# 138 matmuls and 22 transposes, read by nobody, behind a kernel's last used matmul

## The chip, the cores and the metric

The kernel runs on one core of a Trainium2 chip. The metric is the device time of one execution, in microseconds (us). Before the change two runs took 822.97 and 823.05 us, median 823.01 us. TensorE is called PE in the profile (its weight loads PEld), VectorE DVE, ScalarE ACT, GpSimd POOL, and SyncE, which issues the DMAs, SP.

## What is computed

One step of a hybrid transformer layer for a prompt of 1024 positions and for 32 sample positions with a cache of 512, all in float32, width 1024:

```
u = rmsnorm(h, g_pre) @ w_in            # 1024 x 4096: q, k, v and a gate for mixers A and B
oa = band_attention(qa, ka, va)         # 8 heads, chunks of 64, band of 8 + 1 chunks, softmax
ob = stick_breaking(qb, kb, vb)         # 8 heads, causal, products of sigmoids for weights
y = concat(oa * silu(ga), ob * silu(gb)) @ w_out
h = h + rmsnorm(y, g_post)
h = h + sigmoid(h @ w_ple_gate) * (p @ w_ple)
```

Returned are the new h of prompt and sample, and the new keys and values of both mixers. The change adds to none of these.

## The kernel before, in words

The kernel is written as a recording. Calls such as `nc.tensor.matmul` go to a `Recorder` (line 200), which notes each operation with the operations that it must follow. `Recorder.order` (line 307) then plays a model of the five engines. Each engine takes, of its operations that are ready, the one with the lowest key: for TensorE the key is the class `rec.cls` at the time of recording, and then the place in the recording. `Recorder.emit` (line 375) writes the operations in that order; so line 385, the call inside `emit`, is the source line of nearly every instruction in the profile, and the tiles' names tell them apart.

Float32 products are made of pairs: each operand is split into a high part of type float32r and a low remainder, and three float32r products (high x high, high x low, low x high) make one. The work has three stages:

- Normalisation, projection and attention. The columns of `w_in` are taken 128 at a time, against `hnh` and `hnl` (the normalised input, transposed, in three chunks of 352 positions): 24 matmuls of 352 columns for one chunk. These are the groups `mm_qA` to `mm_gB`. Attention is woven between: scores `SA` and `SB`, transposed weights `ptwA` and `ptwB`, values `PVA` and `PVB`.
- The output projection. The 1024 x 1024 product is made by a seven-product scheme on blocks of 512 x 512 (line 1346: `ORDER`, `WHICH`, `LEFT`), four passes over pairs of row tiles (line 1557). `multiply` (line 1414) is one product: 12 matmuls of 512 columns, named `o0P` to `o3P`.
- The gate product with `w_ple_gate`, in the same scheme (`g0P` to `g3P`). Its right-hand blocks are `blocks["g", key]`, float32r tiles of 128 x (2 x 4 x 512): high and low part, four slices, 512 columns. In the last pass the last product, P3 with block `B22`, is cut in two pieces of 256 columns for the second row tile (line 1588, `tail`); their PSUM tiles are `g3P` and `g3P3b`. Behind each piece VectorE adds it to `uu`, `Gate.out` (line 1463) takes the sigmoid, multiplies and adds, and SyncE issues the output DMA.

PSUM tiles come from `psum(tag, name)` (line 408), each one bank of 512 float32 columns. The tags have 2 (`mm`), 3 (`S`), 2 (`T`) and 1 (`PV`) banks. Within a tag the tiles take turns; a new tile must wait for the last use of the one whose bank it takes. `ident` (line 432) is a float32 identity of 128 x 128, which the transposes use.

At the start there are 12 matmuls of 256 columns into a tile `idle` (line 811), whose results nobody reads.

Of the kernel before, what the change touches and what calls it, by code (L numbers as in the profile page):

```python
# [13 lines left out]
P = 128  # L14
# [3 lines left out]
T = SEQ + NS  # L18
# [372 lines left out]
def stream_step(  # L391
# [6 lines left out]
    rec = Recorder()  # L398
    nc = rec
# [8 lines left out]
    def psum(tag, name):  # L408
        return ps.tile([P, 512], F32, tag=tag, name=name, bufs=PS_BUFS[tag])

    def scratch(shape, name):
# [19 lines left out]
    ident = const.tile([P, P], F32, tag="ident", name="ident")  # L431
# [7 lines left out]
        out=maskb, in_=maskb, pattern=[[-1, P]], base=0, channel_multiplier=1,  # L439
# [614 lines left out]
    for n in range(-1, 8):  # L1054
        a = len(order)
        if n < 7:
            ab, p = pairs[n + 1]
# [217 lines left out]
    blocks = {}  # L1275
# [44 lines left out]
    count = [0]  # L1320
# [236 lines left out]
    for m, (nm, src, group) in enumerate(sets):  # L1557
        last_set = m == len(sets) - 1
        state = [{}, {}]
        for n, prod in enumerate(ORDER):  # L1560
            for pair, t in enumerate(group):
# [28 lines left out]
                banks = [bank, psum("S", f"{nm}{t}{prod}b")] if tail else [bank]  # L1590
# [36 lines left out]
                else:  # L1627
                    uu = st.get("uu")
                    if prod in ("P2", "P4") and pair == 0:
                        name = f"cc{m}{prod}"  # L1630
# [31 lines left out]
        if m in (0, 2):  # L1662
# [8 lines left out]
            else:  # L1671
                for q in range(2):
                    g8 = Gate(8, HALF[q])
                    y = short_product(nm, short, q)
                    g8.out(y, at2.tile([P, 512], F32, tag="stg", name=f"o8_{q}", bufs=3))

    rec.emit(tc)


# [33 lines left out]
```

## Time and profile before

| what | value |
|---|---|
| median of two runs | 823.01 us |
| the profiled execution | 822.59 us |
| its span, first to last instruction | 820.8 us |
| PE matmuls, weight loads | 4926 of each |
| granted TensorE clock, mean | 1.000 |
| other engines' busy share | DVE 73%, POOL 62%, ACT 60% |
| HBM traffic | 81.21 MB read, 36.59 MB written |

The page of the profile gives the busy time of each engine, the span in 40 slices, the chain of work that ended last, and the costliest groups of instructions. A matmul's recorded time is longer than the distance to the next one, since matmuls are pipelined; the rate of a group is read from the starts, or from the pieces of the chain, which tile the span. In the timeline "x12" means that 12 instructions of a kind are merged into one row. Between span and device time of the profiled execution lie 1.8 us.

### The profile page before, as it was taken

What the parts mean: (1) busy time and instruction counts of PE and PEld (TensorE: products, weight loads), DVE (VectorE), ACT (ScalarE), POOL (GpSimd) and SP (SyncE); (2) the same over time, 40 slices, a digit from 0 to 9 for tenths busy, and PEclk for the clock granted to TensorE, in tenths of its full rate; (3) what the DMA queues carried; (4) which work ended last, traced back from release to release, by engine and by line L of the source; (5) the groups of instructions that cost most, each with busy time, mean ns of one, the idle gap of its engine ahead of it and who ended that gap; (6) DMA issues with size and microseconds to landing.
All of it is one profiled execution on the core that took longest, in us unless ns stands there. A gap on an engine that the chain in (4) does not pass through costs nothing.

```text
span 820.8 us, 14862 instructions
## 1 busy us (share of the span) xinstructions
PE 811.7 (99%) x4926; PEld 751.1 (92%) x4926; DVE 601.8 (73%) x1197; ACT 496.1 (60%) x1145; POOL 508.3 (62%) x559
## 2 busy tenths in 40 slices
PE   9999999999999999999999999999999999999997
PEld 7999999999999999999999999999998787888786
DVE  6718886776677688898988889985654676686755
ACT  6624745655636667756665775663437966886741
POOL 6526775585766486675657856676463437599513
PEclk9999999999999999999999999999999999999999
DMA  9327544574545563312333233253479847749733
GB/s 309 109 70 249 145 143 146 146 204 146 147 120 171 144 174 96 85 33 67 105 89 82 50 105 92 83 150 111 135 258 303 287 143 243 251 156 362 245 117 128
DMA packets 113279, 127.19 MB, mean 155 GB/s; under 512 B 10850, under 2 KB 80266, under 8 KB 113203
## 3 DMA queue, kind: packets, MB, share of 16 engines
q1 hardware_dynamic: 113202, 126.24, 50.5%
q8 instruction: 39, 0.64, 0.3%
q14 instruction: 38, 0.30, 0.1%
HBM read 81.21 MB, written 36.59 MB: 144 GB/s over the span
## 4 chain that ended last, share of the span: by engine, by line
PE 94%; DVE 2%; POOL 1%; ACT 1%; DMA 1%; issue 0%; SPq 0%; DVEq 0%
PE mm_kB L385 6%; PE mm_gA L385 6%; PE mm_qA L385 6%; PE mm_kA L385 6%; PE mm_gB L385 5%; PE mm_qB L385 5%; PE mm_vA L385 5%; PE mm_vB L385 5%; PE PVB L385 4%; PE SB L385 4%; PE ptwB L385 4%; PE SA L385 4%; PE PVA L385 4%; PE ptwA L385 3%; PE g1P L385 2%; PE o3P L385 2%
## 5 line engine op out<-in xcount | busy, mean ns | idle before, releaser
L385 POOL TENSOR_TENSOR beB<-beB,omB 128x128 f32<-128x128 f32 (+7 forms) x64 | 87.5, 1373 | 78.6 <-DVE omB L385 25.0
L385 DVE TENSOR_TENSOR_SCAN omB<-omB 128x128 f32<-128x128 f32 (+7 forms) x64 | 100.1, 1575 | 4.4 <-ACT omB L385 2.2
L385 POOL TENSOR_SCALAR beA<-beA,statA 128x640 f32<-128x640 f32 (+2 forms) x64 | 44.3, 696 | 48.6 <-DVE statA L385 47.0
L385 ACT CAST wThA<-ptwA 128x128 fp32r<-128x128 f32 (+3 forms) x96 | 40.1, 424 | 37.4 <-PE ptwA L385 36.5
L385 ACT CAST wThB<-ptwB 128x512 fp32r<-128x512 f32 (+3 forms) x96 | 44.9, 487 | 24.7 <-PE ptwB L385 23.2
L385 ACT ACTIVATE omB<-SB 128x384 f32<-128x384 f32 (+5 forms) x96 | 47.4, 507 | 18.9 <-DVE SB L385 8.1
L385 DVE TENSOR_TENSOR wTlB<-ptwB,wThB 128x512 fp32r<-128x512 f32 (+3 forms) x96 | 50.7, 547 | 9.0 <-ACT wThB L385 7.2
L385 DVE TENSOR_TENSOR wTlA<-ptwA,wThA 128x128 fp32r<-128x128 f32 (+3 forms) x96 | 45.6, 485 | 15.7 <-ACT wThA L385 15.0
L385 ACT ACTIVATE beA<-omA,statA 128x640 f32<-128x640 f32 (+2 forms) x64 | 44.7, 699 | 9.4 <-DVE statA L385 3.5
L385 ACT ACTIVATE beB<-SB 128x384 f32<-128x384 f32 (+5 forms) x96 | 46.6, 506 | 3.4 <-DVE Vl2sB L385 2.0
L385 PE MATMUL ptwB<-ident,beB 128*128 128x128 f32 x288 | 45.0, 273 | 0.1
L385 PE MATMUL ptwA<-ident,beA 128*128 128x128 f32 x240 | 41.5, 273 | 0.0
L385 PEld LDWEIGHTS ptwB<-ident,beB 128*128 128x128 f32 x288 | 35.1, 140 | 2.3 <-issue 0.4
L385 PE MATMUL SB<-kdB,LB 128*128 128x384 f32 (+5 forms) x96 | 34.1, 358 | 0.5 <-ACT beB L385 0.5
L385 DVE CUSTOM_DVE_ANT_0 omA<-SA,biasA 128x320 f32<-128x320 f32 (+2 forms) x64 | 30.8, 481 | 4.5 <-PE SA L385 3.8
L385 PE MATMUL SB<-klB,LB 128*128 128x384 f32 (+5 forms) x96 | 33.4, 349 | 0.0
L385 PEld LDWEIGHTS ptwA<-ident,beA 128*128 128x128 f32 x240 | 30.7, 140 | 1.4 <-issue 0.2
L385 POOL TENSOR_TENSOR oB<-oB,oB 128x256 f32<-128x256 f32 x32 | 25.4, 815 | 10.2 <-issue 5.6
L385 PE MATMUL SA<-kdA,LA 128*128 128x320 f32 (+2 forms) x96 | 31.2, 332 | 0.5 <-DVE LA L385 0.4
L385 POOL TENSOR_TENSOR gB<-gB,gB 128x256 f32<-128x256 f32 x32 | 27.5, 878 | 6.3 <-DMA gB<-in_w_ple_gate_dram 6.1
L385 PE MATMUL SA<-klA,LA 128*128 128x320 f32 (+2 forms) x96 | 30.4, 324 | 0.0
L385 POOL TENSOR_TENSOR h<-h,x 128x512 f32<-128x512 f32 (+1 forms) x18 | 23.4, 1320 | 0.8 <-DVE h L385 0.8
(706 smaller groups left out, 2698.1 us busy)
## 6 DMA issues: line engine op xcount, KB each, us to landing
x<-in_x_prompt_dram SPq DMA_DIRECT2D x8, 512.0 KB, 5.5
oB<-in_w_out_dram SPq DMA_DIRECT2D x16, 256.0 KB, 4.5
sum_dro<-oB SPq DMA_DIRECT2D x16, 256.0 KB, 2.2
gB<-in_w_ple_gate_dram SPq DMA_DIRECT2D x16, 256.0 KB, 4.3
sum_drg<-gB SPq DMA_DIRECT2D x16, 256.0 KB, 2.1
x<-in_x_prompt_dram SPq DMA_DIRECT2D x16, 256.0 KB, 3.8
h_dr<-h SPq DMA_DIRECT2D x8, 512.0 KB, 3.5
ht<-h_dr SPq DMA_DIRECT2D x8, 512.0 KB, 5.1
```

The costliest lines, as they stand in the source:

```text
L385: getattr(getattr(tc.nc, o.what[0]), o.what[1])(*args, **kw)
```

## The change

Ahead of `rec.emit(tc)` the recording gets 13 rows of matmuls in class 5, which no other operation has, so that TensorE takes them last. The whole diff:

```
+    rec.cls = 5
+    flat = [blocks["g", key].rearrange("p a k c -> p (a k c)") for key in ("B22", "T1")]
+
+    def twice(name):
+        pt = psum("T", name)
+        for x in range(2):
+            nc.tensor.transpose(pt[:, x * P:(x + 1) * P], ident, ident)
+
+    def row_of(name, n, base=104, step_w=P, step_m=None, banks=1, each=False, count=12, lead=True):
+        if lead:
+            twice("t" + name)
+        out = [psum("mm", f"{name}{x}") for x in range(banks)]
+        step_m = n if step_m is None else step_m
+        for i in range(count):
+            w = flat[0][:, base + step_w * (i % 8):base + step_w * (i % 8) + P]
+            m = flat[1][:, base + step_m * (i % 6):base + step_m * (i % 6) + n]
+            nc.tensor.matmul(out[i % banks][:, 0:n], w, m, start=each or i < banks, stop=each or i >= count - banks)
+
+    row_of("ra", 352)
+    row_of("rb", 352, base=0)
+    row_of("rc", 352, step_w=0)
+    row_of("rd", 352, step_m=0)
+    row_of("re", 352, step_w=0, step_m=0)
+    row_of("rf", 512)
+    row_of("rg", 512, step_w=0, step_m=0)
+    row_of("rh", 384, count=8)
+    row_of("ri", 336, count=8)
+    row_of("rj", 352, banks=2)
+    row_of("rk", 352, each=True)
+    row_of("rl", P, count=2, lead=False)
+    row_of("rm", 352, lead=False)
```

`twice` is two transposes of the identity into one bank of tag `T`; eleven of the rows begin with it. A row is `count` matmuls of `n` columns into one bank of tag `mm` (`rj`: two banks in turn), summed up over the row (`rk`: each on its own, `start` and `stop` set every time). Weights are 128 columns of block `B22`, moved on by `step_w` from one matmul to the next; the moving columns come from block `T1`, moved on by `step_m`; both start at element `base`. That makes 138 matmuls and 22 transposes. Nothing reads the banks, and no output depends on them.

## The prediction

> **What bounds the kernel now.** I read the page first, then the chain of work that ended last over the final 20 us, then the timeline of the end and the waits of the DMA queue's engine there. The changed program's instruction order was read beside them.
>
> ```profile
> span 820.8 us, 14862 instructions
> PE 811.7 (99%) x4926; PEld 751.1 (92%) x4926; DVE 601.8 (73%) x1197; ACT 496.1 (60%) x1145; POOL 508.3 (62%) x559
> PEclk9999999999999999999999999999999999999999
> PE 94%; DVE 2%; POOL 1%; ACT 1%; DMA 1%; issue 0%; SPq 0%; DVEq 0%
> ```
>
> TensorE is busy 99% of the span, makes 94% of the chain, and its granted clock is at the top digit throughout. So work appended to TensorE has no idle time to fall into, except behind the last used matmul. The chain of the last 20 us shows where that is:
>
> ```profile
> 807.65 2.80 PE g3P L385 x12
> 810.44 2.76 PE g2P L385 x12
> 813.20 1.45 PE g3P L385 x12
> 814.65 1.46 PE g3P3b L385 x12
> 816.10 0.02 issue
> 816.13 0.77 DVE uu L385 x2
> ...
> 817.79 0.42 DVE uu L385
> ```
>
> Products of 12 matmuls follow each other without a gap until 816.10; the last two are 256 columns wide. What comes behind them is VectorE's sum, a gate and the output DMA. The end of TensorE's work, and how the five engines fill the rest:
>
> ```profile
> 815.80 0.29 PE L385 MATMUL g3P3b<-gB,wlS4g 128*128 128x256 f32 x1
> 817.08 1.50 SPq L385 DMA_DIRECT2D out_dram<-uu  x3
> ...
> 816.10:820.80 4.70, 0.00 (x0) 0.00 (x0) 2.02 (x5) 0.41 (x2) 0.95 (x1) 1.00 0.33 113
> ```
>
> In the last row the columns are PE, PEld, DVE, ACT and POOL busy: TensorE does nothing in the last 4.70 us. That is the only cover in the kernel for added TensorE work. What closes the program stands in the waits of SyncE from 816 on:
>
> ```profile
> SPq L1709 <- DMA out_dram<-uu: 1.1, 3, 0.4
> SPq L1709 <- PEq L1709: 0.6, 2, 0.4
> ```
>
> SyncE waits for the last output transfers and then twice for the other engines: the program ends with a barrier that all engines, TensorE too, must reach. So matmuls whose results nobody reads still hold the end, once they outlast the transfers.
>
> **The change, part by part.** It adds 138 matmuls and 22 transposes on TensorE, in 13 rows: 11 with two transposes ahead, two (rl, rm) without. It removes nothing. In the built order the 160 stand behind the last g3P3b matmul and ahead of TensorE's closing branch. ACT, DVE, POOL and SP have the same instructions with the same waits in the same order as before; only buffer numbers moved. So there is no added DMA, no step is moved past a queue, and nothing ahead of 815.8 us changes. By width: 96 matmuls of 352 columns (ra to re, rj, rk, rm), 24 of 512 (rf, rg), 8 of 384 (rh), 8 of 336 (ri), 2 of 128 (rl).
>
> Recorded matmul durations overlap (0.29 us for a 256-column one above, but 12 of them in 1.46), so I price by distance from start to start:
>
> ```profile
> 591.07 33.19 PE mm_gB L385 x205
> 552.99 13.41 PE mm_gA L385 x83
> ```
>
> 352 columns: 33.19/205 = 0.1619 us and 13.41/83 = 0.1616 us, each with its own weight load. 96 x 0.1619 = 15.54 us.
>
> 512 columns: 2.76/12 = 0.230 and 2.80/12 = 0.233 by the chain's g2P and g3P rows. I take the middle, 0.2315: 24 x 0.2315 = 5.56 us.
>
> The TensorE page of the Trainium skill ("TensorE: Matmul & The Clock Gate", section "Back-to-back issue gap") gives N / 2.4 + 2.5 ns for one matmul behind another on the warm clock, which would be 149 ns for 352 columns and 216 for 512. This trace does not agree: 162 and 230 to 233. By that rule the whole sum would be an estimated 1.9 us smaller; I keep the trace.
>
> 384, 336 and 128 columns, from these rows of TensorE's timeline:
>
> ```profile
> 339.89 0.31 PE L385 MATMUL SB<-klB,LB 128*128 128x320 f32 x1
> 340.04 0.75 PE L385 MATMUL PVB<-wTlB,v2B 128*128 128x512 f32 x4
> ...
> 343.49 0.34 PE L385 MATMUL SB<-klB,LB 128*128 128x384 f32 x1
> 343.67 0.27 PE L385 MATMUL ptwB<-ident,beB 128*128 128x128 f32 x1
> ...
> 82.30 0.22 PE L385 MATMUL SA<-kdA,LA 128*128 128x128 f32 x1
> 82.36 0.27 PE L385 MATMUL SA<-klA,LA 128*128 128x128 f32 x1
> 82.47 0.53 PE L385 MATMUL mm_kA<-hnh,wl_kA 128*128 128x352 f32 x2
> ```
>
> 384 columns: 343.67 - 343.49 = 0.18; the line between 352 and 512 columns gives 0.176, which I take: 8 x 0.176 = 1.41 us. 336 columns lie between 320 (340.04 - 339.89 = 0.15) and 352 (0.162): 0.154, 8 x 0.154 = 1.23 us. 128 columns: 0.06 and 0.11, so 2 x 0.085 = 0.17 us.
>
> Transposes: a pair of them inside 352-column work shows the cost with what it does to the matmul behind it.
>
> ```profile
> 105.88 0.38 PE L385 MATMUL ptwA<-ident,beA 128*128 128x128 f32 x2
> 106.01 1.05 PE L385 MATMUL mm_qA<-hnl,wh_qA 128*128 128x352 f32 x5
> 106.90 0.38 PE L385 MATMUL ptwA<-ident,beA 128*128 128x128 f32 x2
> ```
>
> From 105.88 to 106.90 there are two transposes and five matmuls: 1.02 - 5 x 0.1619 = 0.21 us a pair. Start to start the pair seems to take only 0.13, but the first matmul behind it starts early and takes longer. 11 x 0.21 = 2.31 us. The lower end for a pair is that 0.13.
>
> Waits: 20 of the added instructions wait on TensorE's own semaphore, because a PSUM bank is used again and its last writer was TensorE. With two banks for each of the two tags, a row waits for the row before the last, finished some two microseconds earlier. Satisfied waits cost nothing that the trace can show: every g2P and g3P product above begins with waits on VectorE or ScalarE, and they follow each other gapless. One wait is short: rm waits for rk, and only rl's two narrow matmuls stand between. The result of a matmul is there when its recorded time ends, 0.32 us after its start (row of x1 below), against 0.17 us of rl plus 0.16 of its own slot; with the semaphore's way and a weight load (0.19) not hidden I put 0.3 us there, bounds 0 and 0.5.
>
> ```profile
> 105.72 0.32 PE L385 MATMUL mm_qA<-hnl,wh_qA 128*128 128x352 f32 x1
> 815.68 0.19 PEld L385 LDWEIGHTS g3P3b<-gB,wlS4g 128*128 128x128 f32 x1
> ```
>
> Sum: 15.54 + 5.56 + 1.41 + 1.23 + 0.17 + 2.31 + 0.30 = 26.52 us of TensorE.
>
> Rows also differ in start address (0 or 104 elements), in whether weights or moving columns stay the same, in the bank and in the start and stop flags. No row of this trace isolates any of these. The spread at one width bounds them: 0.230 to 0.233 (1.4%) at 512 columns with quite different tiles. An unaligned start could cost more than that, the same weights could save something; I allow -3% and +5% on the 138 matmuls (24 us), that is -0.7 and +1.2 us, and take 0.
>
> Where the end goes: the last used matmul starts at 815.80, and 256 columns take a slot of 1.46/12 = 0.12, so the first added one can start at 815.92. 815.92 + 26.52 = 842.44 is the end of the last slot; its result is there 0.16 later, at 842.60. Behind that comes the closing of the program. The barrier is at least the 0.6 us of the SPq row; the upper end is from the last output packet to the span's end. The DMA view of 816 to 820.8, in 40 slices of 0.12 us, shows the last packets in the 30th, at 819.6, so 1.2 us:
>
> ```profile
> DMA  8100000000000000999898999489920000000000
> ```
>
> I take 0.9 and reach 843.5. The output DMA, landed by 819.6, is no longer on the path. So 843.5 - 820.8 = +22.7 us; 3.8 us of the 26.5 are covered by the old tail.
>
> The profiled execution took 822.59 us with a span of 820.8; the same 1.8 us around the new span give 845.3. The median of the runs, 823.01, is 0.4 above the profiled one, which gives 845.7. I predict 845.6 us.
>
> **The rivals.** *Not slower, because unread matmuls do not stay in the program, or do not run.* None of the 160 results is read. If they fell away the time would be 823.0. Against it:
>
> ```profile
> L385 PE MATMUL idle<-newh x12: 415/415/582, 1.3 to 3.8; 128*128 128x256 f32 x12
> ```
>
> These 12 matmuls at the start are read by nobody either, and all 12 ran. The case decides only if some 40 or more of the 160 went away. I give 0.01.
>
> *Within 2%, because the added matmuls run closer together.* 2% of 823.0 is 16.5 us, about what a measurement of this kernel can tell from no change. With 3.8 us covered, the added work would have to take under 20.3 us, 0.77 of my price: 0.125 us for 352 columns. Rows with repeated weights, on an otherwise quiet chip, would be the place. As a floor I take the pace at which transposes, each with a 128 x 128 weight load as well, follow each other in long rows:
>
> ```profile
> 331.55 0.49 PE L385 MATMUL ptwB<-ident,beB 128*128 128x128 f32 x3
> 331.88 0.60 PE L385 MATMUL ptkB<-ident,stkB 128*128 128x128 f32 x4
> ```
>
> Three in 0.33 us, 0.11 each: 138 x 0.11 + 2.31 + 0.30 = 17.8 us, and the time would be 845.6 - 8.7 = 836.9. Against it: 33.19 us for 205 is the rate in a stretch where nothing but these products stands on the chain, and in the tail g2P runs at 0.230 while the other engines are half idle. The Trainium skill's page "TensorE: Matmul & The Clock Gate", section "Back-to-back issue gap", states that a stream of weight loads and matmuls sustains about 131 ns for each of 512 columns, below its own figure for a single one, by which this rival would hold; the trace has 230. I give 0.02.
>
> *Slower than forecast, because waits on TensorE's own semaphore are not free.* If the wait stops TensorE's sequencer so that each of the 20 exposes a matmul's rest (0.32 - 0.16 = 0.16) and a weight load (0.19), that is 20 x 0.35 = 7 us, and the time is 852.6; half of it gives 849. For it: no product in this trace waits for TensorE itself. Against it: the waits are two rows old, and the gapless products. I give 0.07.
>
> **How the numbers follow.** The forecast as summed has 0.90. Its low end: 352 columns at 0.1616, 512 at 0.230, pairs at 0.13, no wait and 0.6 of closing take off 0.03 + 0.04 + 0.88 + 0.3 + 0.3 = 1.5, and addresses 0.7: 843.4. Its high end: 0.233 for 512, the wait at 0.5, 1.2 of closing and 1.2 for addresses add 1.7, 847.3; the range reaches to the first half of the waiting rival, 849. Range 843.2 to 849.0. Slower by over 2% (above 839.5) holds the forecast and the waiting rival, 0.97; the two others make 0.025 for within 2%; faster has no mechanism, 0.005.
>
> **What would show it right or wrong.** The last g3P3b matmul should still start near 815.8 and the last output DMA still land before 820. The timeline should show 13 rows behind it: 352-column rows of 12 with transposes in about 2.15 us (12 x 0.162 + 0.21), the 512-column ones in 2.99, rm starting late by 0.3. TensorE's count should be 5086 and its last matmul end near 842.6. I am wrong if a row is off by over 5% (addresses or weights matter), if idle time stands ahead of the transposes or of a row's first matmul (waits), if the clock falls below 1.00 in the tail, or if the span ends more than 1.2 us behind the last matmul.

## The result, and the profile after

The changed kernel took 848.31 us (median of 848.21 and 848.40) against 823.01, a ratio of 1.0307 with a 95% interval of 1.0263 to 1.0352. The forecast was 845.6, its range 843.2 to 849.0. So it is slower, as forecast, and 2.7 us above the point. The profiled execution took 848.40 us.

Its page, for the span and TensorE's counts:

```profile
span 846.6 us, 15182 instructions
PE 841.1 (99%) x5086; PEld 778.9 (92%) x5086; DVE 601.1 (71%) x1197; ACT 496.5 (59%) x1145; POOL 509.0 (60%) x559
```

All 160 added instructions ran (5086 - 4926), and no other engine has one more. The chain of work that ended last, from the last used product on (start, duration, tile, count; the pieces tile the time):

```profile
817.92 1.44 PE g3P3b L385 x12
819.36 0.22 PE tra L385 x2
819.58 1.94 PE ra L385 x12
821.52 0.22 PE trb L385 x2
821.74 1.94 PE rb L385 x12
823.68 0.22 PE trc L385 x2
823.90 1.94 PE rc L385 x12
825.84 0.22 PE trd L385 x2
826.06 1.93 PE rd L385 x12
827.99 0.22 PE tre L385 x2
828.21 1.94 PE re L385 x12
830.14 0.22 PE trf L385 x2
830.36 2.73 PE rf L385 x12
833.10 0.22 PE trg L385 x2
833.32 2.75 PE rg L385 x12
836.07 0.22 PE trh L385 x2
836.29 1.41 PE rh L385 x8
837.70 0.22 PE tri L385 x2
837.91 1.23 PE ri L385 x8
839.14 0.22 PE trj L385 x2
839.36 1.94 PE rj L385 x12
841.30 0.22 PE trk L385 x2
841.52 1.94 PE rk L385 x12
843.47 0.17 PE rl L385 x2
843.64 2.10 PE rm L385 x12
```

Two things are to be seen. The rows run without a gap from 819.36 to 845.74, which is 26.38 us; the forecast had 26.52. And they begin 3.3 us later than in the trace of before, where g3P3b ended at 816.10. The last used matmul itself:

```profile
819.08 0.29 PE L385 MATMUL g3P3b<-gB,wlS4g 128*128 128x256 f32 x1
```

It starts 3.28 us behind the 815.80 of before, although nothing ahead of it was changed. Its slot of 0.12 and the rows lead to 845.57, the end of rm's slot; its result is there at 845.73, and the span ends at 846.6. SyncE now waits for rm instead of the output DMA, and the two steps of the barrier cost what they did:

```profile
SPq L1742 <- PE rm L385: 23.3, 1, 23.3
SPq L1742 <- PEq L1742: 0.6, 2, 0.4
```

Where the 3.28 us arose is seen when the starts of equal matmuls are laid side by side over both traces: the distance grows to 2.55 us in the first 27 us, jumps by 0.9 near 153 us, and shrinks by 0.2 behind that. The first stretch on TensorE, in before:

```profile
4.07 1.62 PE L385 MATMUL ptp<-ident,pp 128*128 128x128 f32 x8
5.61 1.19 PE L385 MATMUL gpre<-ghl,ones 1*128 1x512 f32 x4
6.73 2.11 PE L385 MATMUL ple<-wph0True,php 128*128 128x512 f32 x8
8.68 1.07 PE L385 MATMUL ple<-wpl0True,php 128*128 128x512 f32 x4
```

and the same four tiles and the next in after:

```profile
4.16 1.94 PE L385 MATMUL ptp<-ident,pp 128*128 128x128 f32 x8
6.03 2.07 PE L385 MATMUL gpre<-ghl,ones 1*128 1x512 f32 x4
8.03 3.78 PE L385 MATMUL ple<-wph0True,php 128*128 128x512 f32 x8
11.61 1.91 PE L385 MATMUL ple<-wpl0True,php 128*128 128x512 f32 x4
13.32 1.49 PE L385 MATMUL ple<-wph1True,php 128*128 128x512 f32 x4
```

Four matmuls of 512 columns stand from 11.61 to 13.32, 0.43 us each; in before they go from 8.68 to 9.59, 0.23 each. By the single starts the pace doubles at 5.2 us in before and at 14.2 us in after. The Trainium skill's page "TensorE: Matmul & The Clock Gate", section "What's actually happening", has a half-rate clock of 1.2 GHz as the state at rest, released by sustained activity; an estimate from that clock, one column a cycle, is 427 ns for 512 columns, and the pace of 0.427 us agrees with it. The view of the granted clock does not show it: it reads 1.00 for this stretch of after too (third column from the end; 10 matmuls where before has 18).

```profile
8.00:12.00 4.00, 4.00 (x10) 3.14 (x10) 1.19 (x3) 2.84 (x5) 1.46 (x4) 1.00 1.03 400
```

That 1.00 is no measurement. The trace of after holds no record of the clock at all; in before the first record, of the full clock, begins at 5.21 us, where the pace doubles. Where there is no record, the view prints 1.00.

The 0.9 us near 153: in after a load of projection weights came late, ScalarE stood 1.40 us at its cast, and the cast behind it held up TensorE's values product.

```profile
153.70 0.62 ACT L385 CAST wh_vA<-wr_vA 128x512 fp32r<-128x512 f32 x1 [1.40 <-DMA wr_vA<-in_w_in_dram]
...
154.92 0.67 PE L385 MATMUL PVA<-wThA,v2A 128*128 128x512 f32 x2 [0.64 <-ACT wThA L385]
```

In before the same cast waited for 0.29 us:

```profile
149.91 0.62 ACT L385 CAST wh_vA<-wr_vA 128x512 fp32r<-128x512 f32 x1 [0.29 <-DMA wr_vA<-in_w_in_dram]
```

So the question for the experiments was whether the 3.28 us belong to the change or to the execution. My theory: to the execution, since the start of the pace differs from one to the next. The rival: a longer program starts slower.

### The profile page after: what moved, and what is told of

It is laid out like the page before. It is cut to its first block, busy times and chain, and to the rows that moved or that the text cites. A ratio compares the mean times of both kernels' runs of the same rounds, so it can differ in the third digit from the quotient of the medians.

```text
span 846.6 us, 15182 instructions
## 1 busy us (share of the span) xinstructions
PE 841.1 (99%) x5086; PEld 778.9 (92%) x5086; DVE 601.1 (71%) x1197; ACT 496.5 (59%) x1145; POOL 509.0 (60%) x559
## 4 chain that ended last, share of the span: by engine, by line
PE 96%; DVE 2%; ACT 1%; DMA 1%; issue 0%; DVEq 0%
PE mm_kB L385 6%; PE mm_kA L385 6%; PE mm_gA L385 5%; PE mm_gB L385 5%; PE mm_qB L385 5%; PE mm_qA L385 5%; PE mm_vA L385 5%; PE mm_vB L385 5%; PE PVB L385 4%; PE SB L385 4%; PE ptwB L385 4%; PE PVA L385 3%; PE SA L385 3%; PE ple L385 3%; PE ptwA L385 3%; PE g1P L385 2%
## 5 line engine op out<-in xcount | busy, mean ns | idle before, releaser
L385 ACT CAST wThB<-ptwB 128x512 fp32r<-128x512 f32 (+3 forms) x96 | 44.9, 486 | 24.3 <-PE ptwB L385 22.7
L385 POOL TENSOR_TENSOR oB<-oB,oB 128x256 f32<-128x256 f32 x32 | 25.5, 818 | 11.6 <-issue 5.7
```

The costliest lines, as they stand in the source:

```text
L385: getattr(getattr(tc.nc, o.what[0]), o.what[1])(*args, **kw)
```

## The experiments

**The changed kernel again, unaltered (no edit).**

> The changed kernel once more, unaltered. In its first profile the last used matmul started 3.28 us later than in the kernel before: 2.55 us of that were lost in the first 25 us, where 512-column matmuls stood 0.427 us apart until 14.2 us (0.23 from 5.2 us on in the kernel before), and 0.8 us behind a weight load that landed late near 153 us. Theory (the start of the clock differs from execution to execution, whatever the program): the times spread over 2 us or more, between about 845.0 (22.6 us above 822.6, the price of the rows alone) and 848.5, and a profile with an early rise of the pace has its last g3P3b matmul near 815.8. Rival (the longer program itself starts slower): all executions near 848.3, within 0.3, and the profile has the slow pace until 14 us again.

Measured: 845.56, 846.19, 847.29 and 848.03 us, beside 21 runs of the kernel before on the same chip from 822.57 to 825.36, median 823.63. The ratio is 1.0277 (1.0263 to 1.0291). The spread is 2.5 us for the changed kernel and 2.8 us for the one before: the theory's case, and the two values each of the first measurement had hidden it. The profile fell on the execution of 847.29, again with the pace slow until 13.9 us, and with the last g3P3b at 817.97; near 151 us nothing came late. The rows took 26.21 us from first to last start, as before.

**One row only.**

```
     row_of("ra", 352)
-    row_of("rb", 352, base=0)
...
-    row_of("rm", 352, lead=False)
```

> Only the first of the 13 rows (two transposes, 12 matmuls of 352 columns, 2.16 us in the first profile). The old tail covers 3.8 us by the prediction, so the row itself costs 0.0 us, and the span ends with the output transfers. Theory (start of the clock varies by execution): 823.0, or up to 826.3 in executions with the late rise. Rival (any lengthening of the program delays the start): 826 in all executions. Rival (the cover is not there, since the closing waits for TensorE first): 825.2 with an early rise.

Measured: 823.35 us, ratio 0.9999 (0.9990 to 1.0008). The row of 2.16 us costs nothing. Its profile has it behind the last used matmul, and SyncE waits for the output transfers at the end, not for TensorE:

```profile
816.83 0.22 PE tra L385 x2
817.05 1.94 PE ra L385 x12
```

```profile
SPq L1730 <- DMA out_dram<-uu: 1.1, 3, 0.4
```

So the cover of the old tail is real for at least these 2.16 us. And the pace rises at 4.8 us in this lengthened program, though it falls back to the slow one from 8.2 to 11.6 us.

**36 unread matmuls at the start, with and without the rows.** Both kernels have this edit; the second is without the change.

```
-    for _ in range(12):
+    for _ in range(36):
         nc.tensor.matmul(idle[:, 0:256], newest[0][:, 0:P], newest[0][:, P:P + 256], start=True, stop=True)
```

> The changed kernel with 36 instead of 12 unread matmuls of 256 columns at the start, so that TensorE is busy without a pause for at least 6 us before its first real work. If a late rise of the pace made the 2.55 us, both kernels with 36 have the fast pace from at most 9 us on, and this one is 22.6 us (26.4 of rows less 3.8 covered) above the kernel with 36 and no rows, within 0.4; a late weight load can add up to 0.9. If the longer program starts slower for another reason, the difference stays 25.3.

> The kernel before with 36 instead of 12 unread matmuls at the start. By itself 0 to 4 us slower than the kernel before, since 24 more matmuls hold up the first transposes by 3 to 5 us and part of that is given back while TensorE waits for the input. Its use is the difference to the changed kernel with 36: 22.6 by the theory that the start made the surplus, 25.3 by the rival that the longer program did.

Measured: 846.25 us with the rows (845.44 to 847.03, five runs) and 823.73 without (822.95 to 824.28, eleven runs), against 823.63 for the kernel before; the ratios to it are 1.0272 (1.0258 to 1.0286) and 0.9996 (0.9987 to 1.0005). The two differ by 22.5 us, where the theory had 22.6 and the rival 25.3. In both profiles the pace is fast from 4.6 and 4.8 us on, and the last g3P3b starts at nearly the same time, with the rows first:

```profile
816.31 0.29 PE L385 MATMUL g3P3b<-gB,wlS4g 128*128 128x256 f32 x1
```

```profile
816.15 0.29 PE L385 MATMUL g3P3b<-gB,wlS4g 128*128 128x256 f32 x1
```

With the start made alike, the surplus is gone. A spread of 1.6 and 1.3 us is left, over fewer runs than the 2.5 and 2.8 above, so the start need not be all of it. The 24 further matmuls, some 3 us of TensorE, cost nothing that can be measured at that place.

**All rows twice.** The second set has the same 13 calls under other names.

```
     row_of("rm", 352, lead=False)
+    row_of("sa", 352)
...
+    row_of("sm", 352, lead=False)
```

> All 13 rows twice, 320 added instructions on TensorE instead of 160. The first set took 26.4 us and 3.8 of it were covered; the second finds no cover left. Theory (price per row, no other cost): rows of 52.7 us together in the profile, the time 48.9 to 49.3 us above the kernel before, that is 872.5 for a median of 823.6, with the same spread of 2 to 3 us from the start. Rival (waits on TensorE's own semaphore grow, or the program's length matters): the second set costs more than 26.4, the time above 874.5.

Measured: 872.25 us beside 823.50, ratio 1.0591 (1.0574 to 1.0609), +48.75 us; the theory had 872.5. From first to last start the rows take 52.42 us in its profile, twice 26.21. The order of a few transposes differs (three pairs of the second set moved ahead of rm), and the price does not.

**2 unread matmuls at the start, no rows.**

```
-    for _ in range(12):
+    for _ in range(2):
```

> The kernel before with 2 instead of 12 unread matmuls at the start, no rows. By the theory that a late rise of the pace made most of the surplus, this kernel has it always late (near 14 us, as in the profiles with 847.3 and 848.4) and its times are near the upper end of the kernel before, 824.5 to 826. Rival (the start is not on the path, because TensorE waits for the input there anyway): the same as before, 823.6.

Measured: 824.93 us (823.32 to 826.38) beside 823.50, ratio 1.0016 (1.0007 to 1.0026). The start is on the path, but the expectation was only half met: the times run from one end to the other, so the rise is not always late, or a late one does not always cost much. In the profile, of an execution of 823.55 us, it came at 10.8 us, and the last g3P3b started at 816.76.

**Single executions of both kernels, unaltered (no edit).**

> The kernel before, unaltered, one look. By the theory the rise of the pace comes early or late with no change to the program: a time near 823 goes with a rise near 5 us and a last g3P3b near 816, a time above 824.5 with a rise near 14 us and a last g3P3b near 818. Rival (the rise is late only in the longer programs): a rise near 5 us whatever the time.

> The same once more, for another look at the start: an early rise with a time near 823, or a late one with a time above 824.5; by the rival always an early one.

> The changed kernel, unaltered, one look. Both of its profiles so far had a late rise of the pace (13.9 and 14.2 us), all seven of other programs an early one or, with 2 unread matmuls, one at 10.8. By the theory an early rise comes here too: then the last g3P3b starts near 816.2, the rows take the same 26.2 us from first to last start, and the time is near 845.5. Rival (this program always rises late): a rise near 14 us and a time above 847.

> The same once more. Early rise and a time near 845.5, or late rise and 847 to 848.4; the rows take 26.2 us from first to last start in either. By the rival always late.

> The kernel before, unaltered, one look at its start. Of 34 of its executions so far the slowest took 825.4 us, 2.8 above the fastest. By the theory a time above 824.5 goes with a rise near 14 us and one near 823 with a rise near 5 us; by the rival the rise is early at any time.

> The same once more: early rise near 823, or late rise above 824.5; by the rival always early.

Measured, with the other profiles of the two kernels; the rows are from first to last start, and the last column is from the start of the last g3P3b to the end of the span:

| execution | us | pace first fast at, us | last g3P3b at, us | rows, us | rest of the span, us |
|---|---|---|---|---|---|
| before, first profile | 822.59 | 5.2 | 815.80 | | 5.01 |
| e7_before_a | 823.09 | 4.2 | 816.30 | | 5.01 |
| e8_before_b | 823.05 | 4.7 | 816.26 | | 5.01 |
| e11_before_c | 823.28 | 6.2 | 816.49 | | 5.01 |
| e12_before_d | 822.93 | 6.5 | 816.14 | | 5.01 |
| after, first profile | 848.40 | 14.2 | 819.08 | 26.21 | 27.55 |
| e1_again | 847.29 | 13.9 | 817.97 | 26.21 | 27.55 |
| e9_again_b | 845.93 | 6.1 | 816.59 | 26.20 | 27.54 |
| e10_again_c | 845.80 | 4.2 | 816.48 | 26.20 | 27.54 |

The last column separates the change from the start. From the last used matmul on, all profiled executions of a kernel take the same time within 0.02 us, and the rows add 22.54 us to it, with an early rise as with a late one. The one row has 5.00 there, so it adds nothing, and the doubled rows 53.76.

The changed kernel has both kinds of start: two late, two early. This row of e10_again_c stands against the 8.03 and 3.78 of the first profile:

```profile
6.36 2.11 PE L385 MATMUL ple<-wph0True,php 128*128 128x512 f32 x8
```

With an early rise it takes 845.8 to 845.9 us, 22.7 above the 823.19 that the kernel before took beside them. So the rival, that this program always rises late, is refuted. The other half was not caught: all five profiles of the kernel before have an early rise, so that its slow executions, up to 825.4 us, are slow for the same reason is likely, and not shown. Nor do the runs decide whether the rows make a late start more frequent: 7 of 41 executions of the kernel before took over 824.5 us, 2 of 11 with one row, 4 of 8 of the changed kernel over 847, and the four with doubled rows lie within 0.7 us of each other. The first fast matmul is not the whole story of the start either: e7 and e8 fall back to the slow pace from 7.7 to 11.1 and from 8.1 to 11.5 us, and yet end near the others.

```profile
7.04 3.23 PE L385 MATMUL ple<-wph0True,php 128*128 128x512 f32 x8 [0.69 <-ACT wph0True L385]
```

The fall-back is where the profile says what the slow pace is. In e7 the matmuls of 512 columns stand 0.427 us apart from 7.94 to 10.92 us, as in the first 14 us of after, and here the granted clock (third column from the end) reads 0.50:

```profile
8.00:10.00 2.00, 2.00 (x6) 1.59 (x5) 0.91 (x2) 0.69 (x1) 0.36 (x1) 0.50 0.98 376
```

So the slow pace goes with a granted clock of one half. The trace's records of the clock say when it changes. Eleven of the fourteen traces have such records, and the first of them begins at the rise: at 5.21 us in before, at 13.67 in e1_again. (The table goes by matmuls, and a fast one may start up to 0.5 us later.) All changes in one execution lie whole steps of 3.41 us apart (the three fall-backs last one step each), and the steps lie differently in each execution.

## Why the prediction was right, and where it was off

- **What bounds the kernel**: right. The chain goes through TensorE to the last row, and the end of the kernel moved by the length of the rows less a fixed cover. One reading was wrong: the granted clock was not at its top throughout, and the mean of 1.000 rests on records that begin at 5.21 us. The prediction's own row of `idle` has a sign of it: 12 matmuls of 256 columns start from 1.3 to 3.8 us, all but the first 0.21 us apart, where the same width stands 0.12 apart in the tail. In e3_after_warm the same matmuls go on at 0.12 us behind the rise.
- **The price of the rows**: right, 26.38 us against 26.52. By term, forecast and measured: 352 columns 15.54 and 15.51 without rm's wait (six rows of 1.94, one of 1.93, and 1.94 for rm); 512 columns 5.56 and 5.48; 384 columns 1.41 and 1.41; 336 columns 1.23 and 1.23; 128 columns and rm's wait together 0.47 and 0.33; transposes 2.31 and 2.42. The errors are small and partly cancel. Within the 0.33 two errors cancel as well, as the waits show.
- **No price for addresses, weights, banks and flags**: right. The rows ra to re, rj and rk lie at 1.93 and 1.94 us each, within one part in 200, and rf and rg at 2.73 and 2.75. Neither start address, nor repeated weights or moving columns, nor two banks, nor start and stop on each matmul shows.
- **Waits on TensorE's own semaphore**: right. Nothing stands between the rows whose bank was last used two rows earlier; only rl and rm together take 0.33 us more than twelve matmuls of 352 columns (0.17 + 2.10 against 1.94). Most of that is no wait. In before, from 82.30 to 82.83, the two narrow matmuls of the prediction and two of 352 columns behind them take 0.53 us; less 2 x 0.162 that is 0.21 us for the narrow pair. The prediction took 0.17, since it left out that the matmul behind them has a longer slot, which it had seen with the transposes. So about 0.1 us is left for the wait, where 0.3 was forecast; no run has rl and rm without the wait. The rival with 7 us is refuted by the chain and by the doubled rows. The row that ends the stretch in before, and rl in after:

```profile
82.83 0.49 PE L385 MATMUL mm_kA<-hnl,wh_kA 128*128 128x352 f32 x2
```

```profile
843.30 0.33 PE L385 MATMUL rl<-gT,gB 128*128 128x128 f32 x2
```

- **The cover and the closing**: right. From rm's result at 845.73 to the end of the span are 0.9 us, as taken. One row of 2.16 us is free, and in the doubled kernel 52.58 - 48.75 = 3.8 us of the rows are covered (52.42 from first to last start and a slot of 0.16), as the forecast said.
- **Unread matmuls fall away, or the added ones run closer together**: both refuted, by 5086 matmuls and by 1.94 us for twelve. The 2% of the second rival is no limit of the measurement: the interval of the one-row kernel is 0.9990 to 1.0008.
- **The step that failed**: "So there is no added DMA, no step is moved past a queue, and nothing ahead of 815.8 us changes." The program ahead of it is the same, but its execution is not. The forecast stood on one profiled execution whose used part ended at 815.80, the earliest of the nine; the first result of the changed kernel came from two executions near the slow end. The missing term is the spread of what lies ahead of the last g3P3b, 0 to 3.3 us there: in the first profile of after 2.55 us from the start and 0.9 from the late load, less 0.2. With the early starts the time is 845.8 to 845.9, and the forecast of 845.6 stands.
- **The range** held for this reason: its upper part had been made for the waits, and what filled it was the start and, in the first profile, one late load. That was luck, and a spread of 2.8 us could have been had only from more executions than the two shown.

Still open is what decides at which step the pace rises. The same program has it at 4.2 and at 14.2 us. In e1_again the steps of 3.41 us back from 13.67 lie at 10.26, 6.84 and 3.43 us; TensorE was at work at each of them, and the pace rose at none. No run varied the kind of work that fills a step.

## What to carry to other kernels

Work appended to the engine that bounds the kernel costs its full pace, measured from start to start in long stretches of the same shape; only what the old tail leaves idle behind that engine's last used instruction is free, here about 4 us. Lay two traces side by side by equal instructions before explaining a difference: a shift that is there before the first changed instruction is not the change's price. Two executions that agree within 0.1 us do not bound the spread; here 21 of them spread over 2.8 us.

## What the runs showed of the hardware

- TensorE's pace at the start of a program differs between executions of one program: twice as slow (0.43 instead of 0.23 us for 512 columns) until 4 to 14 us. It goes with a granted clock of one half: where three executions fell back to it, the clock reads 0.50 for 3.41 us. Ahead of its first record the profile's view prints 1.00, so the pace there is read from the starts. A late rise was worth 1.4 to 2.6 us at 27 us, by which two executions are compared. The Trainium skill's page "TensorE: Matmul & The Clock Gate", section "What's actually happening", explains a varying start by a free-running window of about 3.4 us; the steps of 3.41 us between the records agree, and a rise as late as 14.2 us, behind 13 us of nearly unbroken work, is later than one such window.
- A float32r matmul with its own weight load takes 162 ns for 352 columns and 228 to 233 for 512, whatever the addresses, the repeated operands, the bank or the flags.
- A pair of float32 transposes between such matmuls costs 0.22 us, though from the first start to that of the matmul behind them are only 0.14 us: that matmul has a slot longer by 0.08. Two float32r matmuls of 128 columns cost 0.21 us in the same way.
- A wait of TensorE on its own semaphore costs nothing once the matmul waited for is a row back, and about 0.1 us, by difference, when two matmuls of 128 columns are all that stands between.
